# A reserve on the counted time of the operands of five kinds of lane products, in a two-layer pool, retention and RWKV-7 trunk

## The chip, the cores and the metric

The kernel runs on one core of one Trainium2 chip. The metric is the device time of one execution in microseconds. Before the change it is 2500.98 us, the median of three runs (2497.89 to 2501.22). The profile is of one more execution, which took 2501.75 us.

## What is computed

Two layers act on a sequence of 1024 tokens of width 1024, in float32. Each layer normalises its input, applies a shift and scale from a conditioning vector, and multiplies by one wide input projection. Its columns feed three token mixers, each with a gate path, and three sets of per-channel branch gates.

```python
h = rms_norm(x, norm_g) * (1.0 + scale) + shift
proj = h @ w_in
pool_u, pool_g, q, k, v, ret_g, rw, rw_g, gate_logits = jnp.split(proj, points, axis=-1)
o_pool = causal_pool_mixer(pool_u, pool_w, pool_scale) * jax.nn.silu(pool_g)
o_ret = retention(q, k, v, positions, ret_norm_g) * jax.nn.silu(ret_g)
o_rwkv = rwkv7_time_mix(rw, ...) * jax.nn.silu(rw_g)
y = jnp.einsum('btnw,nwd->btnd', jnp.stack([o_pool, o_ret, o_rwkv], axis=2), w_branch)
merged = jnp.sum(jax.nn.sigmoid(gate_logits.reshape(B, T, 3, D)) * y, axis=2)
return x + gate * (merged @ w_out)
```

The pooling mixer has four groups with trailing windows of 2, 4, 8 and 16 tokens and a 128 x 128 map each. Retention has four heads of 128, in chunks of 128 tokens, with a layer norm per head. RWKV-7 has eight heads of 64 with a recurrent state; its output is normalised per head too. A final RMSNorm follows the second layer.

## The kernel before

Everything is kept transposed, channels on the partitions, tokens along the free dimension in two halves of 512. Each large product is made of three passes of a split into a high and a low part (`mm1`), so one output tile of 128 channels and 512 tokens takes 24 matmuls. These projections are the main stream of TensorE; their PSUM tiles are called acc (three buffers). An item is one output tile for both halves, and `evac` (L1036) takes it out of PSUM and starts what depends on it.

**Lanes.** The mixers are Python generators, kept in queues called lanes: "rwkv" for the RWKV heads (`rwkv_task`, L748), "post" for their normalised outputs (`rwkv_post`, L975), "mix" for pooling and retention (`pool_task`, L616, and `ret_task`, L678, one after another), "norm" and "ada". After each projection matmul `mm1` calls `pump` (L381), which advances each lane whose due time has come. A lane's step emits some instructions and yields a number of nanoseconds until its next step.

**The counted clock.** `clock[0]` counts the time of the emitted TensorE instructions: `mmul` (L404) and `trans` (L413) add to it. `settle` (L328) goes through the instructions emitted on the other engines and counts from a cost formula (`cost`, L314) when each result will be there; it is kept by the tensor's name in `ready`. The formulas know an engine's queue in order of emission, not buffers. `wait(...)` (L374) returns how much later than the counted clock the named operands will be ready, and `advance` (L361) sets the lane's due time from it:

```python
due[k] = max(due[k], clock[0]) + (dt or 0.0)
...
return max(0.0, max(ready.get(n, 0.0) for n in names) - clock[0])
```

So `yield wait(x)` is no wait of the chip. It is a distance in the emitted order, filled by the projection's matmuls. The waits of the chip are semaphores, set by the Tile layer from the data; TensorE takes its instructions in order, and a product that is emitted before its operand is there stops what stands behind it. Outside of the first block, whose order is written out by hand, Tile's scheduler makes the final order of each engine from the order of emission and its own estimates.

**The products that the change touches**, each in a PSUM tile from a pool of two (`mx`, L134; when both have been handed out, `wait` also counts the time at which the older one's reader is done):

- pps (after L647): the map of a pooling group, from pdh and pdl, the two parts of the window mean; they come from ACT and VectorE (DVE). DVE evacuates it into po (L652), which is stored to memory.
- rkv (after L708): keys times values of four chunks, from kt and vt, which ACT copies out of PSUM; DVE makes the states R of it.
- ro (after L722): the retention's output, from the masked scores rsm (called sm), vt and R.
- rot (after L733): four transposes of the normalised output yn, which the helper `layer_norm` makes over DVE, ACT and GpSimd (tile yc, L675); DVE evacuates it into rob, which is stored.
- yt (after L977): the same for RWKV, with yc made by GpSimd; DVE evacuates it into wob, which is stored.

**Buffers.** pdh, pdl, pd, pt, po, kt, vt, rsm, the retention's yc, rob and the evacuated branch gates (gsg) all come from the four buffers of the pool "mo" (L128). RWKV's yc and wob come from the seven of "ri" (L126).

**Order around the lanes.** `plan_layer` (L434) chooses the next item from the state of the lanes: the four heads' RWKV items, retention and pooling items, and between them branch gates that are computed early and stored to memory. Before the branches are merged, `drain("rwkv", "mix")` (L1369) empties the two lanes: it sets the counted clock to each due time and emits the step at once. The weights come by DMA on SyncE's queue (SP) and are split on ACT and GpSimd (`wprep`, L479).

## Time and profile before

| | |
|---|---|
| median of three runs | 2500.98 us (2497.89 to 2501.22) |
| the profiled execution's own time | 2501.75 us |
| its span, first to last instruction | 2499.9 us |
| mean granted clock of TensorE | 0.983 |
| busy, TensorE | 2397.6 us (96%) |
| busy, VectorE | 1357.1 us (54%) |
| busy, ScalarE (ACT) | 791.9 us (32%) |
| busy, GpSimd (POOL) | 822.8 us (33%) |
| read from and written to memory | 174.46 MB, 46.92 MB |

PE is TensorE's matmul, PEld its weight load. In the lines below `rot<-cst,yc` names the written tile and then the read ones; `L417` is a line of the kernel, for matmuls and transposes that of the helper, so products are told apart by their tiles. In the timeline a row has the start, the duration, the engine, the line, the operation, the tiles, the shapes and the count; behind it stands, in brackets, how long the engine was idle before it, and what ended that. PEclk is the share of the full TensorE clock that was granted in a window.

### The profile page before, as it was taken

The page shows a single profiled execution, that of the slowest core. Times are in us where ns is not written, and L with a number is a line of the kernel's source. Part 1 is how long each engine was busy: PE and PEld are TensorE (multiplying, and loading weights), DVE is VectorE, ACT ScalarE, POOL GpSimd, SP SyncE. Part 2 cuts the span into 40 slices and gives each one's busy share as a digit, 9 for nine tenths or more (in the row PEclk, how much of TensorE's full clock was granted, in tenths as well). Part 3 has the DMA queues.
Part 4 walks back from the last instruction along what each step waited for, and adds up shares of the span by engine and source line. Part 5 has one row for each costly group of instructions (what it writes and reads, how often), then busy time and mean ns, then how long its engine had stood idle before and what let it go on. Part 6 is the DMA issues. An engine that isn't in the chain of part 4 may idle for free. (4 is left out here: it accounts for less than half of the span.)

```text
span 2499.9 us, 34854 instructions
## 1 busy us (share of the span) xinstructions
PE 2397.6 (96%) x13312; PEld 1980.1 (79%) x13312; DVE 1357.1 (54%) x2564; ACT 791.9 (32%) x1465; POOL 822.8 (33%) x721
## 2 busy tenths in 40 slices
PE   6989999999999999999999999999999999999998
PEld 4778878877787787887877787788878778787888
DVE  7674566478268443567445646835744664412354
ACT  5532332231332222112444224223322322221243
POOL 4221322232133234454442132322313323236441
PEclk9999999999899999999999999999999999999999
DMA  7131112112113215676431211211211121354342
GB/s 245 54 109 56 43 35 85 36 38 68 47 55 115 75 57 161 193 230 190 136 112 47 68 39 34 77 35 43 86 42 35 61 81 55 123 156 126 102 152 77
DMA packets 124216, 223.68 MB, mean 89 GB/s; under 512 B 14096, under 2 KB 17424, under 8 KB 124048
## 3 DMA queue, kind: packets, MB, share of 16 engines
q1 hardware_dynamic: 124048, 221.44, 28.4%
q8 instruction: 105, 1.72, 0.3%
q14 instruction: 63, 0.52, 0.1%
HBM read 174.46 MB, written 46.92 MB: 89 GB/s over the span
## 5 line engine op out<-in xcount | busy, mean ns | idle before, releaser
L530 POOL TENSOR_TENSOR wl<-wr,wh 128x512 fp32r<-128x512 f32 x342 | 453.6, 1326 | 1189.5 <-ACT wh L529 1108.7
L411 PE MATMUL acc<-hhi,wh 128*128 128x512 f32 x2000 | 809.0, 404 | 14.5 <-DVE k L997 11.1
L411 PE MATMUL acc<-hhi,wl 128*128 128x512 f32 x2000 | 808.5, 404 | 1.7 <-POOL r L991 1.7
L411 PE MATMUL acc<-hlo,wh 128*128 128x512 f32 x2000 | 809.8, 405 | 0.0
L411 PEld LDWEIGHTS acc<-hhi,wh 128*128 128x128 f32 x2000 | 381.1, 191 | 86.5 <-DVE k L997 12.7
L411 PEld LDWEIGHTS acc<-hhi,wl 128*128 128x128 f32 x2000 | 381.4, 191 | 71.7 <-issue 2.2
L411 PEld LDWEIGHTS acc<-hlo,wh 128*128 128x128 f32 x2000 | 381.9, 191 | 68.3 <-issue 0.7
L529 ACT CAST wh<-wr 128x512 fp32r<-128x512 f32 x342 | 211.8, 619 | 680.8 <-PE acc L411 471.5
L411 PE MATMUL acc<-olo,wh 128*128 128x512 f32 x384 | 153.5, 400 | 4.4 <-POOL olo L530 4.3
L411 PE MATMUL acc<-oG,wh 128*128 128x512 f32 x384 | 153.3, 400 | 2.0 <-ACT oG L529 1.0
L411 PE MATMUL acc<-oG,wl 128*128 128x512 f32 x384 | 152.0, 396 | 0.0
L942 DVE TENSOR_TENSOR xst<-cy,MT 64x128 f32<-64x128 f32 x128 | 36.2, 283 | 185.5 <-PE cy L411 185.0
L953 DVE SCALAR_TENSOR_TENSOR S<-ch,pc,SP 64x64 f32<-64x64 f32 x256 | 72.4, 283 | 95.0 <-PE ch L411 86.1
L881 DVE TENSOR_TENSOR MT<-MT,tm 64x30 f32<-64x30 f32 (+14 forms) x240 | 103.9, 433 | 7.5
L939 ACT ACTIVATE SP<-S,pc 128x128 f32<-128x128 f32 x128 | 51.4, 402 | 173.8 <-DVE S L953 169.3
L875 DVE TENSOR_TENSOR tm<-MT 64x30 f32<-64x30 f32 (+14 forms) x240 | 101.3, 422 | 7.5
L948 DVE COPY Z<-ch 64x128 f32<-64x128 f32 x128 | 36.1, 282 | 117.7 <-PE ch L411 117.3
L411 PEld LDWEIGHTS acc<-olo,wh 128*128 128x128 f32 x384 | 73.2, 191 | 22.6 <-POOL olo L530 6.6
L411 PEld LDWEIGHTS acc<-oG,wh 128*128 128x128 f32 x384 | 72.9, 190 | 20.9 <-ACT oG L529 2.0
L1457 DVE SCALAR_TENSOR_TENSOR gs<-gs,acc 128x512 f32<-128x512 f32 x64 | 43.5, 683 | 82.8 <-PE acc L411 71.7
L411 PEld LDWEIGHTS acc<-oG,wl 128*128 128x128 f32 x384 | 73.1, 190 | 16.8
L411 PEld LDWEIGHTS ch<-xst,G 128*128 128x128 f32 x512 | 76.7, 191 | 11.6 <-DVE xst L942 0.5
(273 smaller groups left out, 3643.8 us busy)
## 6 DMA issues: line engine op xcount, KB each, us to landing
wr<-in_w_all SPq DMA_DIRECT2D x364, 256.0 KB, 2.7
gd<-gsg SPq DMA_DIRECT2D x80, 256.0 KB, 2.0
gs<-gd SPq DMA_DIRECT2D x80, 256.0 KB, 2.9
wada<-in_w_ada SPq DMA_DIRECT2D x70, 256.0 KB, 3.1
ol<-od SPq DMA_DIRECT2D x64, 256.0 KB, 3.0
ringG<-in_w_ada SPq DMA_DIRECT2D x26, 256.0 KB, 5.2
x<-in_xT SPq DMA_DIRECT2D x16, 256.0 KB, 4.9
od<-po SPq DMA_DIRECT2D x16, 256.0 KB, 2.3
```

The lines of the kernel that those rows point to most:

```text
L411: nc.tensor.matmul(out, lhsT=lhsT, rhs=rhs, start=start, stop=stop, **kw)
L529: nc.scalar.copy(hi, src)
L530: eng.tensor_tensor(lo, src, hi.bitcast(F32), op=ALU.subtract)
L875: nc.vector.tensor_tensor(pr, M3[:, i + 1 :, i : i + 1].to_broadcast([64, n, i]), M3[:, i : i + 1, 0:i].to_broadcast([64, n, i]), op=ALU.mult,
L881: nc.vector.tensor_tensor(M3[:, i + 1 :, 0:i], M3[:, i + 1 :, 0:i], pr, op=ALU.add)
L939: nc.scalar.activation(SP, S, AF.Copy, scale=pcc)
L942: nc.vector.tensor_tensor(xst[0:64, :], cy[0:64, 0:P], AV[:, c * P : (c + 1) * P], op=ALU.add)
L948: nc.vector.tensor_copy(Z[0:64, c, :], ch[0:64, 0:P])
L953: nc.vector.scalar_tensor_tensor(Sn[rw, rw], ch[rw, P + 64 * hd : P + 64 * hd + 64], pc[rw, c : c + 1], SP[rw, rw], op0=ALU.mult, op1=ALU.add,
L1457: nc.vector.scalar_tensor_tensor(s, s, 1.0, ps, op0=ALU.add, op1=ALU.mult)
```

## The change

`wait` takes a reserve, `spare`, in nanoseconds, which is added to the latest counted time of the named operands; the time of the older PSUM buffer gets none. Five calls give one: 2500 ahead of pps, 1000 ahead of rkv, 1500 ahead of ro, 3000 ahead of rot and 3000 ahead of yt. All other calls leave it at zero.

```diff
-    def wait(*aps):
+    def wait(*aps, spare=0.0):
         settle()
         names = [x.tensor.name if hasattr(x, "tensor") else x.name for x in aps]
+        t = max(ready.get(n, 0.0) for n in names) + spare
         if len(mxq) == 2:
-            names.append(mxq[0])
-        return max(0.0, max(ready.get(n, 0.0) for n in names) - clock[0])
+            t = max(t, ready.get(mxq[0], 0.0))
+        return max(0.0, t - clock[0])
...
-            yield wait(dh, dl)
+            yield wait(dh, dl, spare=2500)
             ps = mx("pps")
...
-            yield wait(kt, vt)
+            yield wait(kt, vt, spare=1000)
             kv = mx("rkv")
...
-            yield wait(sm, vt, *(x for x in R if x is not None))
+            yield wait(sm, vt, *(x for x in R if x is not None), spare=1500)
             ops = mx("ro")
...
-            yield wait(yn)
+            yield wait(yn, spare=3000)
             ps = mx("rot")
...
-        yield wait(yn)
+        yield wait(yn, spare=3000)
         ps = mx("yt")
```

## The prediction

> **What bounds the kernel now.** I read the page first, then the waits of TensorE (PE), then the timeline and the stage windows around the longest of them, and last the chain that ended last.

> ```profile
> span 2499.9 us, 34854 instructions
> PE 2397.6 (96%) x13312; PEld 1980.1 (79%) x13312; DVE 1357.1 (54%) x2564; ACT 791.9 (32%) x1465; POOL 822.8 (33%) x721
> ```

> PE is busy for 2397.6 of 2499.9 us; no other engine passes 54%. Time can come from two places only: the 102.3 us in which PE stands idle, and stretches in which it works slowly. The waits of PE say what ends the idle time (engine, tile, line; who was waited for; us in total, times, longest):

> ```profile
> PE rot L417 <- DVE yc L675: 17.0, 10, 3.7
> ...
> PE acc L411 <- DVE k L997: 11.1, 3, 4.2
> ...
> PE nps L411 <- ACT ksh L774: 4.2, 5, 1.5
> PE pps L411 <- ACT pdh L529: 4.1, 1, 4.1
> PE yt L417 <- POOL yc L675: 4.0, 2, 2.5
> PE pps L411 <- ACT MT L902: 3.9, 1, 3.9
> PE acc L411 <- ACT gsg L1070: 3.4, 2, 2.8
> ...
> PE pps L411 <- DVE pdl L530: 2.9, 1, 2.9
> PE nps L411 <- DVE bv L857: 2.8, 1, 2.8
> ...
> PE yt L417 <- DVE ksq L787: 0.7, 1, 0.7
> ...
> PE rkv L411 <- ACT rvt L706: 0.6, 1, 0.6
> ...
> PE ro L411 <- DVE G L848: 0.5, 1, 0.5
> ...
> PE ro L411 <- DVE ksq L787: 0.3, 1, 0.3
> ```

> Five products of the lanes are the ones whose wait gets a reserve: rot 17.0, pps 4.1 + 3.9 + 2.9 = 10.9, yt 4.0 + 0.7 = 4.7, rkv 0.6, ro 0.8. That is 34.0 us, a third of PE's idle time. The nature of such a wait is seen at the longest rot:

> ```profile
> 801.49 1.11 PE L417 MATMUL rot<-cst,yc 128*128 128x128 f32 x4 [3.69 <-DVE yc L675]
> ...
> 802.83 0.63 PE L411 MATMUL acc<-hhi,wl 128*128 128x512 f32 x1
> 803.26 0.63 PE L411 MATMUL acc<-hhi,wh 128*128 128x512 f32 x1
> ```

> PE takes its instructions in order. The transposes stood in its stream 3.69 us before DVE had finished yc, and the projection's matmuls (acc), whose operands were there, stood behind them. After the wait comes a second cost: acc matmuls now start 0.43 us apart. The stage windows give the clock there (window, length; PE busy, weight loads, DVE, ACT, POOL; then PEclk):

> ```profile
> 581.90:585.40 3.50, 2.78 (x9) 2.39 (x10) 3.36 (x6) 0.00 (x0) 3.04 (x4) 0.51 0.34 94
> 626.30:640.00 13.70, 12.11 (x82) 9.35 (x83) 1.45 (x2) 4.96 (x9) 2.55 (x2) 0.50 0.28 90
> 800.40:807.30 6.90, 5.81 (x16) 4.75 (x17) 6.69 (x12) 0.40 (x1) 4.46 (x4) 0.51 0.47 149
> 824.30:827.70 3.40, 3.30 (x8) 2.66 (x9) 3.12 (x10) 0.64 (x2) 0.00 (x0) 0.50 0.41 154
> 2022.30:2029.20 6.90, 6.16 (x15) 4.82 (x16) 6.49 (x17) 0.58 (x1) 0.00 (x0) 0.51 0.11 37
> 2148.60:2155.50 6.90, 4.95 (x17) 4.20 (x17) 5.08 (x6) 0.60 (x1) 1.36 (x2) 0.51 0.42 153
> 348.00:355.00 7.00, 7.00 (x41) 6.12 (x42) 5.72 (x10) 2.00 (x3) 0.52 (x1) 1.00 0.24 75
> ```

> ```profile
> 151.80:155.30 3.50, 2.90 (x8) 2.38 (x9) 2.77 (x6) 2.42 (x4) 0.10 (x1) 0.51 0.38 144
> ```

> At a granted clock of 0.5 half of PE's busy time is lost. Which waits stand ahead of these windows:

> ```profile
> 152.41 0.80 PE L411 MATMUL pps<-pdh,pw 128*128 128x512 f32 x1 [4.09 <-ACT pdh L529]
> ...
> 347.96 0.66 PE L417 MATMUL rot<-cst,yc 128*128 128x128 f32 x4 [1.97 <-DVE yc L675]
> ...
> 582.62 1.11 PE L417 MATMUL rot<-cst,yc 128*128 128x128 f32 x4 [2.89 <-DVE yc L675]
> ...
> 627.89 0.79 PE L411 MATMUL pps<-pdh,pw 128*128 128x512 f32 x1 [3.91 <-ACT MT L902]
> ...
> 2023.04 0.80 PE L411 MATMUL pps<-pdl,pw 128*128 128x512 f32 x1 [2.90 <-DVE pdl L530]
> ...
> 2147.82 0.66 PE L417 MATMUL yt<-cst,yc 128*128 128x128 f32 x4 [2.50 <-POOL yc L675]
> ...
> 2150.65 1.09 PE L417 MATMUL rot<-cst,yc 128*128 128x128 f32 x4 [1.95 <-DVE yc L675]
> ```

> Of the half-clock windows shown, every one but that at 824.3 is opened by one of the five products: waits of 2.89 to 4.09 us, or 2.50 and 1.95 close together. A single 1.97 us wait (at 347.96) leaves the clock at 1.00.

> **The change, part by part.** No instruction is added or removed, and no semaphore wait either. A lane yields how long its next step should stay un-emitted; the change adds 1.0 to 3.0 us to that number ahead of five kinds of product. While the counted clock runs through the reserve, the projection's matmuls are emitted; at full clock one acc matmul starts about 0.43 / 2 = 0.22 us after another, so 3 us are some 14 of them. They take the places ahead of the product, and the same work does the waiting. So each wait loses the smaller of itself and its reserve.

> rot (reserve 3.0): 17.0 us in ten waits. Two of them do not move, those of layer 0's last retention task: at the merge the lanes are drained, which sets the counted clock to the due time and emits at once, with no matmul put in between:

> ```profile
> 961.48 0.66 PE L417 MATMUL rot<-cst,yc 128*128 128x128 f32 x4 [0.36 <-DVE yc L675]
> ...
> 977.57 0.66 PE L417 MATMUL rot<-cst,yc 128*128 128x128 f32 x4 [1.78 <-DVE yc L675]
> ```

> 17.0 - 0.36 - 1.78 = 14.9, and of the 3.69 us 0.7 stay: 14.2 us. pps (2.5): three waits, each longer than the reserve, so 3 x 2.5 = 7.5 us. yt (3.0): 4.7 us whole. rkv (1.0) and ro (1.5): 0.6 + 0.8 = 1.4 us. Together 14.2 + 7.5 + 4.7 + 1.4 = 27.8 us.

> Clock: what stays of the pps waits is 1.59, 1.41 and 0.40 us and of the rot wait 0.69, all under the 1.97 us that left the clock alone. So the windows they opened go: (2.78 + 12.11 + 5.81 + 6.16 + 4.95) / 2 = 15.9 us, and 2.90 / 2 = 1.5 us at 151.8. The upper sum is 27.8 + 15.9 + 1.5 = 45.2 us.

> [...]

> What the change costs. The lanes get longer in counted time: 5.5 us a retention half, 2.5 a pool half, 3.0 a normalised half of RWKV. Their own next steps (the evacuation on DVE, the store on SP's queue) move by as much, past weight loads and gate stores on that queue; what they store is read after the merge or behind a drain. The end does not hang on the lanes: the chain goes from the last rot straight into projections,

> ```profile
> 2171.80 0.66 PE rot L417 x4
> 2172.46 84.91 PE acc L411 x371
> ```

> so 11 us more of the last retention task are covered by 84.9 us of ready matmuls. Without that cover they would cost up to 11 us.

> What is late next: other products of the same stages. In the rows above the waits for k, ksh, bv and gsg make 11.1 + 4.2 + 2.8 + 3.4 = 21.5 us. While PE stood at a rot, the other engines caught up; without the stand PE reaches its next products earlier by that much. Between nothing and a doubling I take half, 11 us.

> Buffers: yc, pdh, pdl, kt, vt and rsm live in the four "mo" buffers that gate evacuations (gsg) use too, and the count does not know of buffers:

> ```profile
> 626.10 0.62 ACT L529 CAST pdh<-pd 128x512 fp32r<-128x512 f32 x1 [13.59 <-DMA gd<-gsg]
> ```

> ```profile
>   POOL pt L629: 22.4, 4
> ...
>   PE pps L411: 3.7, 1
> ```

> The first row is a split on ACT waiting for a gate's store; the other two, from the view of the tile gsg, are gate evacuations on ACT waiting for pool steps (us, times). Holding buffers 1 to 3 us longer makes some evacuations late, and the accumulators behind them. One such event is the 2.8 us of the gsg row with its half-clock window (824.3: 3.30 / 2 = 1.65), 4.4 us. Bounds are none and one for each of the 16 pool halves (70 us); since today's 22.4 us of ACT waiting cost PE only 3.4, I take two, 9 us. Last, the first pps (152.41) may not move: its place among the other lanes' products is also set by the scheduler that makes the final order from its own estimates, and an operand 4.09 us late may be late for a reason that moves along; half of its 2.5 + 1.5 us goes off, 2 us.

> 45.2 - 11 - 9 - 2 = 23 us. The profiled execution took 2501.75 us (span 2499.9 and 1.85 around it), 0.8 above the median of the runs, 2500.98; the gain is taken off the median: 2478.

> **The rivals.**

> 1. The lateness moves on. A product's lateness is DVE's or ACT's being behind, and the next product in the stream pays it. For: the rows of nps and of k have the same character and get no reserve. Against: the projection that fills the reserve is work which DVE and ACT need only after a whole item. It gives back all 21.5 us once more, with the two buffer events and the first pps: 45.2 - 21.5 - 9 - 2 = 13 us, 2488; at worst 2496.

> 2. The order doesn't change. The scheduler places instructions by its own estimates, and where these put the operand later than the emission, a later emission moves nothing. For: a reserve is no wait on the chip. Against: ten rot waits mean that those estimates are too early too. Time: 2501.

> 3. Slower: buffers. The held pool buffers make gate evacuations late and PE waits for an accumulator, 4.4 us each time. Against 45.2 us it decides from the eleventh event on; with all 16 pool halves it is 70 - 45 = 25 us slower, 2526. For: the gsg rows above. Against: only 3.4 us of them reach PE today, and the reserve adds no buffer, only time.

> **How the numbers follow.** About 0.2%, 5 us, is what a measurement of this kernel can tell from no change (the runs reach from 2497.89 to 2501.22). Forecast, 2456 to 2484: 0.55. Rival 1, 2484 to 2496: 0.20. Rival 2, 2496 to 2506: 0.10. Rival 3, above 2506: 0.15. The predicted time is 2478. The lower end is the whole 45 us, 2456; the upper end, 2506, leaves out rival 3. Faster: 0.55 + 0.20 = 0.75; same: 0.10; slower: 0.15.

> **What would show it.** Right: rot, yt and pps together under 10 us in PE's waits (32.6 now), rot with one or two rows beyond the drained pair; fewer half-clock windows, a higher mean granted clock; PE's busy share up. Rival 1: the waits for k, ksh, bv and gsg, 21.5 us now, grow past 32. Rival 2: the five products keep their rows. Rival 3: acc waits for gsg, 2 to 3 us at a time, ten times or more, each followed by a half-clock window. I am wrong in the mechanism if the lanes' waits go and the span doesn't, with no other wait grown.

## The result, and the profile after

The changed kernel takes 2492.50 us (median of 19 runs, 2480.34 to 2515.86) beside 2508.99 us of the kernel before on the same chip (19 runs). The ratio is 0.9944 [0.9922, 0.9965]: faster by 0.56%, some 14 us, where 23 were forecast. The profiled execution took 2492.5 us; that of before took 2501.75. In the five sets of runs of the experiments below the kernel before has medians of 2499.9 to 2503.2 us; the changed one was not run there. In e1_pd_wait two of the twelve executions were in a slower state; its row below has the other ten.

Of the page after:

```profile
span 2490.6 us, 34861 instructions
PE 2398.2 (96%) x13312; PEld 1981.5 (80%) x13312; DVE 1364.1 (55%) x2564; ACT 792.0 (32%) x1465; POOL 821.0 (33%) x721
```

PE's idle time fell from 102.3 to 2490.6 - 2398.2 = 92.4 us, by 9.9. Its busy time did not move (2397.6 before, 2398.2 now). Time won back from half-clock windows would have to show in the busy time: in the profile before, acc matmuls start 0.43 us apart at half clock (from 803.26 on) and 0.23 apart at full (from 807.86 on). The mean granted clock is 0.983 in both executions. So all that this execution gained is idle time. Each engine does as many instructions as before; the seven more in the span are records of semaphores (2609 of them, 2602 before).

The waits of PE after (engine, tile, line, who was waited for: us in total, times, longest):

```profile
PE acc L412 <- DVE k L998: 12.5, 3, 5.5
PE rs L412 <- DVE rob L739: 5.4, 2, 3.5
PE acc L412 <- POOL olo L531: 5.3, 6, 1.3
PE nps L412 <- ACT ksh L775: 4.7, 4, 1.4
PE acc L412 <- ACT gsg L1071: 4.7, 2, 4.1
PE acc L412 <- ACT hhi L1172: 4.1, 6, 1.5
PE bt L418 <- DVE BK L813: 3.8, 3, 2.6
PE nps L412 <- DVE ksl L777: 3.4, 4, 2.7
PE nps L412 <- DVE bv L858: 2.8, 1, 2.8
PE rot L418 <- DVE yc L676: 2.7, 1, 2.7
PE pps L412 <- ACT pdh L530: 2.6, 1, 2.6
PE ro L412 <- DVE G L849: 1.1, 1, 1.1
PE pps L412 <- ACT BKt L837: 0.9, 1, 0.9
PE rkv L412 <- DVE wob L983: 0.4, 1, 0.4
```

and those rows of before, not shown yet, that have grown:

```profile
PE acc L411 <- POOL olo L530: 4.3, 4, 2.7
PE acc L411 <- ACT hhi L1171: 3.3, 6, 0.7
PE nps L411 <- DVE ksl L776: 1.4, 3, 0.8
PE bt L417 <- DVE BK L812: 1.0, 1, 1.0
```

The five products with a reserve wait 2.7 + 2.6 + 0.9 + 1.1 + 0.4 = 7.7 us, 34.0 before: 26.3 us are gone, yt's rows whole. Of these, 26.3 - 9.9 = 16.4 came back at other products: rs 5.4 (no row before), BK +2.8, ksl +2.0, k +1.4, gsg +1.3, olo +1.0, hhi +0.8, ksh +0.5, together 15.2.

**Where the clock went.** The clock record of the trace lists each half-clock window. Here they are by the wait of PE that falls into the 3.4 us ahead of them, in us of half clock (the last window, which runs to the end, left out):

| ahead of the window | before | after |
|---|---|---|
| the five products | 151.9, 581.9, 626.3, 800.4, 2022.4, 2148.7: 40.9 | 974.3 (a drained rot): 3.4 |
| rs | none | 759.2, 1950.5: 6.8 |
| nps, bt | none | 138.0, 1725.2, 1776.4: 10.2 |
| gsg | 824.3: 3.4 | 810.4: 6.8 |
| k | 13.6 | 13.6 |
| the merges (oG, olo) | 10.2 | 10.2 |
| the kernel's start | 35.8, 56.3: 6.8 | none |
| no wait at all | 216.7: 3.4 | 827.5 (23.9 long), 1844.7: 27.3 |
| sum | 78.3 | 78.3 |

The windows that the prediction said would go did go, but as many us came elsewhere, the largest part of them behind no wait. That window, and what lies ahead of two others, in slices of 3.41 us (start and end; length; PE busy, weight loads, DVE, ACT, POOL; then PEclk):

```profile
807.03:810.44 3.41, 0.72 (x4) 0.26 (x2) 3.18 (x11) 0.00 (x0) 0.00 (x0) 1.00 0.00 1
820.69:824.10 3.41, 3.41 (x16) 2.56 (x14) 0.75 (x1) 0.95 (x2) 3.03 (x3) 1.00 0.33 127
824.10:827.51 3.41, 3.41 (x69) 2.89 (x69) 2.27 (x2) 2.07 (x5) 1.60 (x2) 1.00 0.59 189
827.51:851.40 23.89, 23.89 (x154) 18.02 (x154) 0.16 (x1) 4.53 (x8) 1.27 (x1) 0.50 0.07 18
1947.09:1950.50 3.41, 1.51 (x11) 1.10 (x10) 3.38 (x7) 1.82 (x4) 0.00 (x0) 1.00 0.37 127
```

From 820.69 on PE is never idle, and yet the clock is at 0.50 from 827.51 for 23.89 us. The rows of the tile m, the 32 x 32 products of RWKV's triangular inverse, show what fills the slice ahead:

```profile
824.10:827.51 3.41, 2.39 (x64) 2.16 (x64) 0.70 (x2) 1.00 0.59 189
```

In the timeline these are two groups, with three acc matmuls between them:

```profile
824.14 1.19 PE L412 MATMUL m<-MT,G 32*32 32x32 f32 x32
...
826.15 1.19 PE L412 MATMUL m<-MT,G 32*32 32x32 f32 x32
```

**Two numbers for each run.** Below, a run's full-clock time is its span times the mean granted clock, and its clock loss is the rest of the span. In the 19 runs of the changed kernel the full-clock time is 2448.3 us with a standard deviation of 1.9 (2445.3 to 2452.3), while the loss goes from 27.3 to 67.9, median 42.3; span and clock correlate at -0.986. So the scatter of these 19 runs is nearly all clock loss, and it differs from execution to execution of one kernel. Two limits of these numbers: the clock of a run is listed to 0.001, which is 2.5 us here, and the loss counts PE's idle time inside a window too (87.1 us of windows in the profile before, 68.7 of them busy). In the sets of runs of before that list each run's clock, the full-clock time has medians of 2458.1 to 2460.2 and the loss of 40.0 to 42.5. Against these the change is worth 10 to 12 us of full-clock time, and nothing of clock. But the 19 runs of before on the chip of the changed kernel list no clocks. With a full-clock time of 2458 to 2460 us their median of 2508.99 would hold a loss of 47 to 49 us, by this estimate 5 to 7 above that of the changed kernel. Whether some us of clock were won on that chip is not shown.

### The profile page after: what moved, and what is told of

It is laid out like the page before. It is cut to its first block, busy times and chain, and to the rows that moved or that the text cites. A ratio compares the mean times of both kernels' runs of the same rounds, so it can differ in the third digit from the quotient of the medians.

```text
span 2490.6 us, 34861 instructions
## 1 busy us (share of the span) xinstructions
PE 2398.2 (96%) x13312; PEld 1981.5 (80%) x13312; DVE 1364.1 (55%) x2564; ACT 792.0 (32%) x1465; POOL 821.0 (33%) x721
## 4 chain that ended last, share of the span: by engine, by line
PE 77%; DVE 10%; issue 2%; POOL 2%; ACT 1%; DMA 1%; SPq 0%; DVEq 0%; POOLq 0%; ACTq 0%
PE acc L412 61%; PE cy L412 3%; PE ch L412 3%; DVE MT L882 2%; DVE tm L876 2%; PE av L412 2%; PE m L412 2%; PE g L412 1%; PE ro L412 1%; DMA wada<-in_w_ada 1%; POOL olo L531 1%; PE rs L412 1%; PE bt L418 1%; PE rkv L412 1%; DVE MT L866 1%
## 5 line engine op out<-in xcount | busy, mean ns | idle before, releaser
L412 PE MATMUL acc<-hhi,wh 128*128 128x512 f32 x2000 | 809.8, 405 | 17.2 <-DVE k L998 12.5
L530 ACT CAST wh<-wr 128x512 fp32r<-128x512 f32 x342 | 211.7, 619 | 678.5 <-PE acc L412 466.5
L412 PE MATMUL acc<-oG,wl 128*128 128x512 f32 x384 | 151.9, 397 | 0.0
L412 PEld LDWEIGHTS acc<-olo,wh 128*128 128x128 f32 x384 | 73.0, 190 | 23.9 <-POOL olo L531 8.0
L412 PEld LDWEIGHTS acc<-oG,wl 128*128 128x128 f32 x384 | 73.4, 191 | 16.8
L412 PEld LDWEIGHTS cy<-Z,G 128*128 128x128 f32 x512 | 76.8, 190 | 11.4
```

Source lines behind the costliest of these rows:

```text
L412: nc.tensor.matmul(out, lhsT=lhsT, rhs=rhs, start=start, stop=stop, **kw)
L530: nc.scalar.copy(hi, src)
```

## The experiments

Each kernel was run in five rounds beside the kernel before (6 to 12 executions of each). Where an expectation names theories by letters, D is the loss of clock at RWKV's inverse, G the gate evacuation that stands behind the pooling split on ACT; the lateness that moves on and the held buffers are the prediction's first and third rival. Medians, ratios and the two numbers:

| label | us | ratio to before | full-clock time | clock loss (range) |
|---|---|---|---|---|
| a1_rot_only | 2523.76 | 1.0082 [1.0053, 1.0112] | 2457.3 | 65.6 (55.4-73.4) |
| a2_pps_only | 2516.35 | 1.0053 [1.0030, 1.0076] | 2455.9 | 59.1 (45.0-75.8) |
| c2_yt | 2502.76 | 0.9992 [0.9974, 1.0010] | 2462.3 | 40.0 (34.9-45.1) |
| c1_rkv_ro | 2503.83 | 1.0006 [0.9981, 1.0031] | 2459.3 | 42.5 (37.5-65.6) |
| a3_yt_rkv_ro | 2493.54 | 0.9964 [0.9944, 0.9985] | 2446.3 | 44.8 (37.3-60.1) |
| a4_five_by_300 | 2505.91 | 1.0010 [0.9988, 1.0032] | 2457.9 | 47.6 (40.0-60.4) |
| b3_double | 2482.07 | 0.9912 [0.9875, 0.9948] | 2442.6 | 39.7 (32.1-47.3) |
| b1_rs_reserve | 2499.33 | 0.9963 [0.9927, 0.9998] | 2447.0 | 50.0 (32.2-70.4) |
| b5_rs_older | 2488.79 | 0.9939 [0.9914, 0.9964] | 2451.8 | 34.8 (27.3-52.5) |
| e1_pd_wait | 2503.24 | 0.9992 [0.9963, 1.0020] | 2449.6 | 50.0 (34.8-70.5) |
| e3_double_pd | 2502.65 | 0.9988 [0.9963, 1.0012] | 2448.5 | 53.8 (39.8-70.5) |
| d0_spread_alone | 2493.33 | 0.9956 [0.9935, 0.9977] | 2457.1 | 34.9 (27.4-37.5) |
| d1_spread_inverse | 2501.60 | 0.9989 [0.9968, 1.0009] | 2460.4 | 40.0 (34.9-45.0) |
| d3_rot_only_spread | 2501.46 | 0.9980 [0.9963, 0.9997] | 2461.2 | 37.5 (32.4-42.5) |
| d4_tight_alone | 2506.52 | 1.0014 [0.9992, 1.0036] | 2456.1 | 47.6 (42.5-73.2) |
| d5_double_spread | 2514.51 | 1.0042 [1.0023, 1.0061] | 2469.4 | 42.7 (42.7-47.8) |
| f1_m_spread | 2491.01 | 0.9961 [0.9942, 0.9980] | 2457.6 | 29.9 (27.4-34.9) |
| f2_av_spread | 2529.87 | 1.0103 [1.0079, 1.0127] | 2469.9 | 58.1 (47.9-65.8) |

### The reserves one by one

a1_rot_only keeps the reserve of rot alone; the other four are 0.

```diff
-            yield wait(dh, dl, spare=2500)
+            yield wait(dh, dl, spare=0)
...
             yield wait(yn, spare=3000)
```

> The reserve of 3.0 us on rot alone; the other four at zero. Theory A (each reserve takes away its own product's waits, a part comes back at the next products of the same lane and engines, and the granted clock differs from run to run whatever the order): PE's waits at rot fall from 17.0 to under 4 us, the wait of rs for DVE's rob, which the changed kernel has for 5.4 us and the one before has not, is here too (3 to 6 us), and span times clock, 2457 us in the profile before, falls by 3 to 8 us. Theory B (the gain is that of a reshuffled order, not of the reserves): span times clock moves by any amount up to 10 us either way, and the rs wait has no tie to the reserve on rot. Theory C (the reserves end the clock losses, as predicted): the windows at half clock behind rot are gone and their sum falls from 87 to below 75 us.

It is slower than before. Of its waits of PE:

```profile
PE acc L412 <- ACT gsg L1071: 8.8, 2, 5.3
PE pps L412 <- ACT pdh L530: 4.5, 2, 2.6
PE pps L412 <- DVE pdl L531: 4.2, 2, 2.8
PE rs L412 <- DVE rob L739: 3.4, 1, 3.4
PE m L412 <- ACT MT L903: 3.0, 2, 1.6
PE rot L418 <- DVE yc L676: 2.8, 3, 1.8
```

rot is down to 2.8, as the mechanism has it. But gsg, rs and m pay, the full-clock time hardly moves, and the loss is 23 us above that of before. It has two long half-clock windows, each at an inverse, one of 27.3 us at 2050.2 and this one:

```profile
841.80:865.70 23.90, 23.46 (x153) 18.26 (x154) 0.75 (x1) 5.54 (x10) 1.89 (x2) 0.50 0.19 56
```

a2_pps_only keeps the 2500 of pps alone.

```diff
             yield wait(dh, dl, spare=2500)
...
-            yield wait(yn, spare=3000)
+            yield wait(yn, spare=0)
```

> The reserve of 2.5 us on pps alone. Theory A: PE's waits at pps fall from 10.9 to about 3.5 us, those at rot stay at 14 to 20, rs does not wait for rob, and span times clock falls by 3 to 8 us. Theory B: any amount up to 10 us either way. Theory C: the three windows behind pps (3.4, 13.7 and 6.8 us) are gone and the time falls by 7.5 us of idle and 10 us of clock.

pps still waits 8.9 us, where 3.5 were expected, in two rows where there were three, and rot keeps its wait, 17.8:

```profile
PE rot L418 <- DVE yc L676: 17.8, 11, 2.9
...
PE pps L412 <- DVE pdl L531: 4.9, 1, 4.9
...
PE pps L412 <- ACT pdh L530: 4.0, 1, 4.0
```

The first pps row of the prediction is among them: 4.05 us ahead of 152.57, and 4.06 with a reserve of 5.0 us (b3_double, below). In a1, a3, c1 and c2, which give pps none, it is 2.59 to 2.61. So the reserve does not decide this wait. rs waits 1.3 us for rob here, though rot has no reserve. The loss is high once more, with windows of 30.7 and 23.9 us at the inverse.

c2_yt keeps the 3000 of yt alone, c1_rkv_ro those of rkv and ro (1000 and 1500), a3_yt_rkv_ro the three together. The diff of a3 (the other two set 0 at one or two lines more; the last line is yt's):

```diff
-            yield wait(dh, dl, spare=2500)
+            yield wait(dh, dl, spare=0)
...
-            yield wait(yn, spare=3000)
+            yield wait(yn, spare=0)
...
         yield wait(yn, spare=3000)
```

> The reserve on yt alone (3.0 us). The three reserves on yt, rkv and ro together gave 2446.3 us of span times clock against 2458.1, though the waits of these three products had only 6.1 us before. Theory A (own waits only): yt's 4.7 us go, span times clock 2452 to 2455. Theory B (what moves is the order of the later steps on DVE, so other waits move as well): rot and pps waits change by 3 us or more in sum without a reserve of their own.

> The reserves on rkv (1.0 us) and ro (1.5 us) alone. Before, their waits were 1.4 us in all. If the parts add up, the three reserves on yt, rkv and ro (2446.3 us of span times clock) less that on yt alone (2462.3 against 2459 before) leave all of the gain to these two: span times clock 2440 to 2448. If the order of a combination makes it (Theory B): 2452 to 2462, and the parts do not add up here either.

> The reserves on yt (3.0 us), rkv (1.0) and ro (1.5), none on rot and pps. Theory A: PE's waits at yt, rkv and ro fall from 6.1 to under 2 us, rot and pps keep theirs (28 us, with a few us of shift), and span times clock falls by 0 to 5 us; the time is the same as before within 0.3%. Theory B: any amount up to 10 us either way. Theory C: the window at 2148 is gone, 2.4 us more.

In full-clock time against before, yt alone is 3.2 us slower, rkv and ro change nothing (-0.6), and the three together win 11.8. Rot alone gives 0.8 and pps 2.2. The parts, -0.8 - 2.2 + 3.2 - 0.6, make nothing of the 10 us of the whole. So the gain is no sum of terms of the reserves. Nor do the waits keep to the products that have one: in a3 rot and pps wait 13.4 + 5.3 = 18.7 us without a reserve, and 18.5 in c2_yt, where before has 27.9 (theory A of a3 had them at 28, theory B of c2 moved by 3 or more). Each reserve shifts the other lanes' places, and what PE meets there decides.

The reserves can also move the order of the projection's own items, since `plan_layer` goes by the lanes' state. In the order in which acc is evacuated, by the names of the written tiles, some items did move in the changed kernel. That alone does not make the gain: a3 and c1 have one and the same order, and only a3 wins.

How a gate becomes late is seen in c2_yt, in the timeline of DVE, ACT and PE:

```profile
609.88 1.91 DVE L886 STREAM_TRANSPOSE MT<-MT 32x1024 f32<-32x1024 f32 x1
611.70 3.75 DVE L891 STREAM_TRANSPOSE G<-MT 32x1024 f32<-32x1024 f32 x2
615.48 0.69 DVE L637 SCALAR_TENSOR_TENSOR pd<-pt,pu 128x512 f32<-128x512 f32 x1
616.20 0.62 ACT L530 CAST pdh<-pd 128x512 fp32r<-128x512 f32 x1 [14.63 <-DVE pd L637]
616.73 0.59 ACT L1071 ACTIVATE gsg<-acc 128x512 f32<-128x512 f32 x1
...
617.37 0.80 PE L412 MATMUL acc<-hhi,wh 128*128 128x512 f32 x1 [8.12 <-ACT gsg L1071]
```

DVE takes pd after 5.7 us of transposes of the inverse. The split of pd waits for it on ACT, the gate's evacuation stands behind the split in ACT's stream, and PE waits 8.12 us for the accumulator. None of these rows waits for a buffer.

### More and less of the reserve

a4_five_by_300 has 300 in place of each reserve; b3_double doubles all five.

```diff
-            yield wait(dh, dl, spare=2500)
+            yield wait(dh, dl, spare=5000)
...
-            yield wait(yn, spare=3000)
+            yield wait(yn, spare=6000)
```

> All five products with a reserve of 0.3 us: the emitted order changes a little in the same places, but no wait of 2 to 4 us can be covered. Theory A: the sum of PE's waits at the five products falls by at most 0.3 us a wait, from 34 to 28 or more, span times clock stays within 5 us of before, the time is the same within 0.2%. Theory B (a reshuffle is enough): it comes out as far from before as the changed kernel does, 9 us or more, in one direction or the other. Theory C: the half-clock sum stays at about 87 us.

> All five reserves doubled (5.0, 2.0, 3.0, 6.0, 6.0 us). Theory A: the five products' waits fall from 7.8 to under 3 us (the drained rot stays), but the later evacuations make others wait as much or more; span times clock 2445 to 2453. Theory F (the third rival of the prediction: held buffers make gate evacuations late): the waits of acc for gsg grow from 4.7 to 9 us or more and the time is 5 to 15 us above the changed kernel's.

With 300 nothing is won, the five products still wait 31.2 us, and acc is evacuated in the order of before. The doubled reserves are the fastest version of the study, 0.9912: full-clock time 2442.6, loss 39.7. Its page and waits:

```profile
PE 2383.8 (96%) x13312; PEld 1973.2 (80%) x13312; DVE 1363.6 (55%) x2564; ACT 791.4 (32%) x1465; POOL 819.7 (33%) x721
```

```profile
PE acc L412 <- DVE k L998: 18.5, 3, 10.2
...
PE rs L412 <- DVE G L849: 5.9, 1, 5.9
```

There is no row of acc waiting for gsg: with the reserves doubled no gate is late for PE. That speaks against the prediction's third rival. k has 18.5 us where it had 11.1. The five products wait 10.7 us, more than the 7.7 of the change, where under 3 were expected, and PE's idle time is 2475.2 - 2383.8 = 91.4 us, hardly less than 92.4. So what this execution gains over the change is nearly all clock (granted clock 0.987, 0.983 there), and not shorter waits.

### The new wait of rs, and the gates

rs waits because its PSUM tile is the one that rot had, and DVE evacuates rot late. b1_rs_reserve gives rs a reserve on its operands; b5_rs_older counts one on the PSUM tile.

```diff
-            yield wait(kT[h], qT[h])
+            yield wait(kT[h], qT[h], spare=3000 * h)
```

```diff
-            t = max(t, ready.get(mxq[0], 0.0))
+            t = max(t, ready.get(mxq[0], 0.0) + older)
...
-            yield wait(kT[h], qT[h])
+            yield wait(kT[h], qT[h], older=3000 * h)
```

> The changed kernel with a reserve of 3.0 us also ahead of the second half's rs, the product that follows rot in the lane. Theory A (what rot, pps and yt no longer wait for comes back at the next product whose operand or PSUM buffer hangs on the same late engines): the rs wait of 5.4 us falls below 1.5, and span times clock from 2448.3 to 2442 to 2446 if nothing else grows. Theory B (reshuffle): rs falls as well, and span times clock ends anywhere from 2440 to 2458.

> The changed kernel, with 3.0 us added for the second half's rs to the counted time of the older PSUM buffer. The reserve on rs's operands had left its two waits for rob as they were, 3.5 and 1.9 us, since k and q had long been there. Theory A: the wait is for the PSUM buffer that rob empties, so both waits fall below 1 us, and span times clock to 2443 to 2447. Theory B: rs's waits fall but others grow by as much; span times clock 2447 to 2455.

The first changes nothing at rs (still 5.4, where under 1.5 was expected): its operands are long there, and a reserve counts from what comes last. The second takes the waits of rs away (under 1 us), and others pay, gsg above all:

```profile
PE acc L412 <- ACT gsg L1071: 11.8, 3, 7.5
```

Its full-clock time is 3.5 us above that of the change.

e1_pd_wait moves the pooling split to 2.5 us of counted time after its input; e3_double_pd does that to the doubled reserves.

```diff
             yield 2400
+            yield wait(d, spare=2500)
             dh, dl = t_mo("pdh", F32R)[:, 0:HF], t_mo("pdl", F32R)[:, 0:HF]
```

> The changed kernel with one more reserve: the split of the pooling mean into pdh and pdl is emitted 2.5 us after the counted time of pd, in place of a fixed 2.4 us after pd's own emission. Theory G (the projection waits for gsg because ACT, in order, holds the gate evacuation behind a split whose input stands behind the inverse on DVE): the waits of acc for gsg fall from 4.7 to below 1 us and span times clock from 2448 to 2440 to 2446. Theory B (waits only change places): gsg falls, other waits grow by as much, span times clock 2446 to 2455.

> The kernel with doubled reserves (2482.1 us, span times clock 2442.6, waits for gsg under 1 us) and the same reserve ahead of the split. Theory G: there is nothing left for it to take away, span times clock stays within 3 us of 2442.6 and the time within 6 us of 2482. Theory B: it moves by more than 4 us in either direction.

gsg's longest wait falls from 4.1 to 2.3, but there are four of them and their sum is 6.7, where under 1 was expected. With the doubled reserves the kernel loses 6 us of full-clock time, and k waits 21.1. Putting the split off cures single waits, not the sum.

### The clock at the inverse

d0_spread_alone has no reserves and puts more matmuls between the groups of small products of the inverse, m (32 x 32) and av (64 x 64). d1_spread_inverse does it with the reserves of the change, d3_rot_only_spread with that of rot alone, d5_double_spread with the doubled ones; d4_tight_alone has no reserves and takes distance away (100 and 0).

```diff
                 if u % 16 == 15:
-                    yield 600
+                    yield 1800
...
-            yield 400
+            yield 1600
```

> The kernel before (all reserves zero) with longer steps in the 64x64 inverse of each RWKV head: 1800 in place of 600 ns after each group of the small m products, 1600 in place of 400 ns after each group of av, so that 5 to 7 more acc matmuls stand between two groups. Theory D (the long half-clock windows of 14 to 31 us come where PE is fed these small products close together: once a wait has dropped the clock there, it stays low until the projection's matmuls are dense again): no window of over 10 us in the profile, span times (1 - clock) falls from a median of 42.5 us by 5 to 12 us, and span times clock stays at 2458 within 5 us. Theory E (long windows are chance, or follow the length of the wait alone): the median loss stays within 4 us of 42.5 and long windows remain.

> The changed kernel with the same longer steps in the inverse. Theory D: no window of over 10 us (the changed kernel has one of 23.9 us), the loss to the clock falls from a median of 42.3 us to 28 to 37, span times clock stays at 2448 within 5 us; 5 to 12 us faster than the changed kernel. Theory E: same as the changed kernel within 4 us.

> The reserve on rot alone, as in the run that came out at 2523.8 us with a loss to the clock of 65.6 us, and the longer steps in the inverse (1800 and 1600 ns). Theory D (long half-clock windows live in the closely fed inverse): the loss falls by 20 us or more, to 33 to 42 us, no window of over 11 us, and the time to 2490 to 2505. Theory E (the loss of the rot-only kernel comes from its own waits: gsg 8.8, k 13.5, rs 3.4 us): the loss stays above 55 us.

> The kernel before, all reserves zero, with shorter steps in the inverse: 100 in place of 600 ns after a group of m products, none in place of 400 ns after a group of av, so that fewer acc matmuls stand between the groups. Theory D: the loss to the clock rises from 40 to 42 us to 48 or more and long windows of 14 us or more stand at several of the eight inverses. Theory E: the loss stays within 4 us of 42, or follows the sum of the waits.

> Doubled reserves and the longer steps in the inverse. Theory D: the loss to the clock falls from the 39.7 us of the doubled reserves to 33 to 37 and no window of over 11 us stands at an inverse. What the longer steps do to the waits is open: with all reserves at zero they left span times clock as it was (2457.1), with the reserves of the change they cost 12 us (2460.4); 2443 to 2460 here.

Rot alone with the spread loses 37.5 us in place of 65.6, the spread alone 34.9 where before has 40.0 beside it, tight groups 47.6, where 48 or more were expected (with windows of 20.5 and 23.9). The same stage in d0, from the first m to the last av, all work and then that of acc:

```profile
860.50:887.00 26.50, 26.50 (x264) 20.91 (x263) 1.34 (x2) 8.73 (x15) 3.82 (x3) 1.00 0.33 107
```

```profile
860.50:887.00 26.50, 18.28 (x72) 12.56 (x71) 0.00 (x0) 2.34 (x4) 1.00 0.33 107
```

and in the changed kernel:

```profile
823.60:851.40 27.80, 27.80 (x224) 21.09 (x223) 2.43 (x2) 7.11 (x13) 3.38 (x3) 0.57 0.13 39
```

```profile
823.60:851.40 27.80, 14.84 (x32) 8.26 (x31) 0.00 (x0) 0.74 (x2) 0.57 0.13 39
```

In 26.50 us at full clock the inverse and 72 projection matmuls are done, in 27.80 us at 0.57 the inverse and 32. But d1 and d5 show that the spread isn't free: the lane gets longer, waits come back elsewhere (olo 11.9, gsg 11.2 and oG 9.2 in d5), and the full-clock time rises to 2460.4 and 2469.4. A loss of 28 to 37 was expected for d1 and of 33 to 37 for d5; they are 40.0 and 42.7, though no window is over 10.3 us in either.

Which of the small products it is was open until two last runs. f1_m_spread is the change with 1800 between the m groups alone, f2_av_spread with 1600 between the av groups alone (each has one half of the diff above).

> The changed kernel with 1800 in place of 600 between the groups of 32x32 products (m) of the RWKV inverse; the av groups keep their 400. Theory of the pairs of m: with TensorE never idle the clock falls only where two groups of m lie in one slice of 3.41 us, and with some 1.8 us of counted time between them no slice holds two. So no half-clock window stands without a wait ahead of it, none at the inverse is longer than 10.3 us, and the clock loss (span times one minus the granted clock) scatters by under 20 us over the executions (40 us in the changed kernel: 27 to 68), with a median of 33 to 41 (42.3). Theory of the whole inverse (m and av alike): the av groups, still 400 apart, open long windows too, so the scatter stays over 30 us. The full-clock time is expected between 2446 and 2462 by both, since the lanes get longer and the waits come elsewhere.

> The changed kernel with 1600 in place of 400 between the groups of 64x64 products (av) of the RWKV inverse; the m groups keep their 600. Theory of the pairs of m: the windows without a wait still open in part of the executions, two m groups in a slice ahead of them, but they end earlier since the av groups have more acc matmuls between them: at most 17 us in place of 24. The clock loss scatters by over 20 us and its median lies between 36 and 46 (42.3 before this edit). Theory of the whole inverse: spreading either part helps alike, and the scatter falls under 20 us here too.

f1: loss 29.9, the least of all kernels, and its nine runs scatter by 7.5 us, where 19 of the changed kernel scatter by 40; no window without a wait, none at the inverse over 10.2 us. (The scatter alone proves little: c2_yt, not spread, has 10.2 in twelve runs.) The median is even lower than expected (33 to 41). f2: two windows stand behind no wait (627.4 and 2088.3), the longest at the inverse has 17.1, and the loss is 58.1, above the expected 36 to 46; its scatter, 17.9, is just short of the 20 expected. So the two parts are not alike. Some of f2's windows stand behind long waits, 8.1 us for k among them, so its loss says little of av; that the windows without a wait stand behind m groups is shown by the slices in the next section, for all 19 windows that follow a slice with PE over 0.90 busy. f1 also has waits that came back (gsg 10.3, k 15.4): its full-clock time is 2457.6, about that of before, and its ratio, 0.9961, no better than the change's.

## Why the prediction was wrong

The direction was right; of the 23 us forecast the profiled pair has 9.3, and the runs some 14. 2492.50 lies outside the forecast of 2456 to 2484, in the range of the first rival. By its steps:

- **The waits of the five products: right in sum.** 27.8 us were to go, 26.3 went. Rot, yt and pps together have 2.7 + 3.5 = 6.2 us, under the 10 named. That each wait loses the smaller of itself and its reserve is borne out by rot (17.0 to 2.8 in a1). For pps it is luck: with its own reserve alone it keeps 8.9 of 10.9, and without one it has 5.2 to 5.4 in a3, c1 and c2 (8.7 in a1). The doubt about the first pps was in place: it keeps 2.6 of its 4.1.
- **What is late next: right in size, wrong in place.** The idle part of the sum was 27.8, less 11 for the products behind, 2 x 2.8 for buffers and 1.25 for the first pps, 9.9. Measured: 102.3 - 92.4 = 9.9. But k, ksh, bv and gsg grew only from 21.5 to 12.5 + 4.7 + 2.8 + 4.7 = 24.7, far from the 32 of the first rival. The most part is rs, a product of the same lane, whose PSUM tile waits for rot's evacuation, and BK and ksl. So the first rival's mechanism, that the next product pays, is the better part of what happened, at other products than it named. That the sum agrees is luck: the parts of the change do not add up to it.
- **The clock term: this is the step that failed.** "So the windows they opened go" was right; that the 17.4 us are then won was not. Of 17.4, less 3.3 and 0.75 taken off for the buffers' windows and the first pps, 13.3 us were to come back. The table of windows shows 37.5 us of half clock gone at the five products, and 37.5 come: 23.9 at pairs of m groups, 10.2 at nps and bt, 6.8 at rs, 3.4 at gsg, less the 6.8 at the kernel's start, which are missing in this execution. So this execution has 0 of the 13.3. In the medians of the runs the loss is 42.3 against 40.0 to 42.5; at most the 5 to 7 us estimated above came back.
- **Order unchanged (second rival): refuted** by the waits. **Held buffers (third): not borne out**; in b3_double no acc waits for gsg. The longest gate wait of the changed kernel stands behind the pooling split, whose input is late on DVE, as in c2_yt:

```profile
810.64 0.62 ACT L530 CAST pdh<-pd 128x512 fp32r<-128x512 f32 x1 [10.62 <-DVE pd L643]
811.17 0.59 ACT L1071 ACTIVATE gsg<-acc 128x512 f32<-128x512 f32 x1
...
811.81 0.79 PE L412 MATMUL acc<-hhi,wh 128*128 128x512 f32 x1 [4.06 <-ACT gsg L1071]
```

Why windows come at other places can be read from the 20 traces (before, after and the 18 experiments). In each of them all half-clock windows begin on one grid of 3.413 us: in the profile after, 827.5 - 138.0 = 689.5 us are 202 such steps, 1950.5 - 138.0 are 531. Counted from the start of the span, the grid lies at 1.67 us in the profile before and at 1.49 in that after. I fitted the grid to the ends of the windows in each trace (steps of 3.4133 us) and cut PE's records into its slices, from 160 us on and up to 30 us before the end. For a slice at full clock, what follows it:

| PE executes, share of the slice | slices | followed by half clock |
|---|---|---|
| under 0.40 | 118 | 118 |
| 0.40 to 0.45 | 36 | 33 |
| 0.45 to 0.60 | 121 | 28 |
| 0.60 to 0.90 | 487 | 19 |
| over 0.90, m and av under 0.60 of the slice | 12096 | 0 |
| over 0.90, m and av over 0.60 of the slice | 219 | 19 |

In the last row, all 19 are among the 66 slices in which m alone has 0.60 or more, that is, two groups: 16 of the 17 at 0.68 to 0.70, 3 of the other 49. The 147 slices in which av alone has 0.60 or more opened none. In the five kernels with the m groups spread, no slice has 0.60 of m, and none of their 3082 slices at full clock with PE over 0.90 busy was followed by half clock. From a slice at half clock with PE busy over 0.90, the clock came back in all 195 cases with less than 0.2 of m and av, and in 15 of 114 with more. So in these traces half clock followed 151 of the 154 slices in which PE executed for less than 0.45, and 16 of the 17 full ones with m at 0.68 to 0.70; and a window that reached the inverse mostly went on there, in 99 of the 114 slices with 0.2 or more of m and av.

This shows what the prediction took wrongly from its rows. The length of a wait alone does not tell whether a window follows. In the slice with the wait of 1.90 us at rs (1947.09, above) PE was busy for 1.51 of 3.41, a share of 0.44, and the clock fell. In that with rot's 1.97 us of the kernel before,

```profile
346.41:349.82 3.41, 1.86 (x15) 1.78 (x16) 3.41 (x6) 0.02 (x1) 0.94 (x1) 1.00 0.30 77
349.82:353.23 3.41, 3.41 (x17) 2.81 (x16) 3.38 (x7) 0.80 (x1) 0.00 (x0) 1.00 0.20 77
```

it was busy for 1.86, 0.55, and the clock stayed. So 1.97 us, which the prediction read as a limit, was none: 1.90 us was followed by half clock, with more of its slice idle. The windows of one profile are one draw, as the loss of 27.3 to 67.9 us in 19 runs of one kernel shows, and a term built from them belongs to that draw.

What stays open: why the three reserves of a3, all five, and the doubled ones win 10 to 18 us of full-clock time, while single ones win next to none. Each is a new order of the same work, and I found no term that gives it. Whether the reserves save clock once the m groups are apart isn't settled either: d1 loses more than d0 (40.0 against 34.9), f1 less (29.9). A fifth buffer in the pool "mo" was not tried.

## What to carry to other kernels

What a wait taken away is worth is what the next late operands leave of it: here 26.3 us of PE's waits made 9.9, and single parts made nothing or a loss, so run the parts and the whole, and don't add. Before a clock term goes into a sum, split the runs into span times clock and the rest: in the 19 runs here the first was steady to 2 us (its standard deviation is 1.9) and the second moved by 40 us, so don't take the windows of one profile for those of the kernel. Look at stretches where TensorE is busy with small products: here two groups of 32 x 32 in a slice of 3.41 us, 0.68 to 0.70 of it, were followed by half clock in 16 of 17 cases, in the profile after for 23.89 us, and with 1.2 us more of counted distance between the groups (f1_m_spread) there were no such windows, at a price in full-clock time (2448.3 to 2457.6).
